# Extra products of constants ahead of the first pair's products in the recurrence's preparation

## The chip, the cores and the metric

The kernel runs on one core of a Trainium2 chip. The metric is the device time of one execution in microseconds, the median of several runs. The kernel before took 3859.59 us (median of 3 runs, 3859.28 to 3872.24).

## The reference, cut to what matters

The reference is one inference step of a two-layer trunk for 1024 prompt tokens and 8 samples of 16 tokens, 1024 features. Layer 0 is an RWKV-7 layer: projections of the mixed input, a recurrence over time per head, an output projection, then a SwiGLU feed-forward. Layer 1 is attention over a band of chunks with a second feed-forward. The change touches the recurrence alone:

```python
def step(s, inp):
    r_t, w_t, k_t, v_t, a_t, b_t = inp
    sa = jnp.einsum('bhij,bhj->bhi', s, a_t)
    s = s * w_t[:, :, None, :] + sa[..., None] * b_t[:, :, None, :] + v_t[..., None] * k_t[:, :, None, :]
    y = jnp.einsum('bhij,bhj->bhi', s, r_t)
    return s, y
```

The 1152 tokens are 3 blocks of 384. A block is 3 windows of 128 tokens (w = 0 to 8; window 8 holds the samples), and a window has 16 heads of 64, taken as two halves of 8 heads (hf = 0, 1).

## The kernel before

The step by step recurrence is computed in chunks of 64 tokens: within a chunk, products of all pairs of tokens are formed, masked, and a triangular system is solved. `proj(b)` makes the projections of block b (`proj_lora`, `proj_k`, `proj_r`, `proj_v`) and, in between, `inverses(b)`, which solves the triangular systems of its three windows. `windows(us)` runs the recurrence. Its units are taken in pairs, the two halves of one window: `prep(i)` calls `win_prep` for both units of pair i, then `win_run` runs their states, `win_y` and `win_post` make the output, and the next pair is prepared. For block b > 0, `layer0a` alternates five steps of the windows of block b-1 with four of `proj(b)` (line 1195); for the last block the windows 6, 7, 8 alternate with the output projection and the adaLN products (`ada_steps`, lines 1202 to 1206). So the first pair of a block (windows 0, 3 and 6) is prepared while the next block's `proj_lora` runs, whose gate products (`gates`, line 595, tiles `acc<-ag`) are followed by a sigmoid on ACT and a scan on DVE (line 607). Window 6's pair is prepared beside the end of block 2's `proj_v` and the first output projections.

`win_prep(w, hf)` loads the operands (XL, and BK, which has one buffer, so that the next unit's load waits until this unit has been read), and does three things on PE, all into banks called G, of which there are two. For each chunk c of 2 it takes two banks, one per row half e, and writes 4 pairwise products of 128 columns into each (line 842); DVE masks them out of the banks (lines 845, 847). Then it takes two banks more and transposes BK into them (line 856); ACT copies these to BKT (line 858). All are fp32. The operands of e = 0 lie in rows 0 to 63, those of e = 1 in rows 64 to 127.

Other names that the steps use: `acc<-mx` are the large projection products of 384 columns, `st` the banks of the solver's merges and of the states, `aux<-raw,scT` the adaLN products, whose weights (`raw<-in_wada`) come by POOL's queue, `cst` the constants' tile of 916 columns (identity, block ones, ones, masks), `st<-y,cst` the 128x512 fp32 products of `win_post` (lines 1058 and 1062), `Z<-T` and `TT<-Z` the DMAs of the solver.

The order of the instructions on an engine isn't that of the Python text: `TileContext(nc, schedule_with_timeline_sim=True)` orders them by a simulated timeline within their dependences. An instruction more at one place moves others.

Of the kernel before, what the change touches and what calls it, by code (L numbers as in the profile page):

```python
# [137 lines left out]
def mm(nc, out, lhsT, rhs, start, stop):  # L138
    return nc.tensor.matmul(out, lhsT, rhs, start=start, stop=stop)  # L139


class Trunk:
# [631 lines left out]
    def st(self, tag, shape, bufs=1, dt=F32):  # L774
        return self.pp.tile(shape, dt, tag=tag, name=self.nm(tag), bufs=bufs)

    def win_first(self, w, hf, ld):

        nc = self.nc
        b, wi = divmod(w, 3)  # L780
        fs = slice(4 * hf, 4 * hf + 4)
        pa = self.wt("pa", [128, 2, 8, 64], 1)
        for i, n in enumerate(("kk", "b")):
            nc.sync.dma_start(pa[:, i], self.sp[b][n][:, wi, fs, :].rearrange("p f (c t) -> p (f c) t", t=64))
        G = self.bank("G", 2)
        for c in range(2):
            for f in range(4):
                for e in range(2):
                    h = slice(64 * e, 64 * e + 64)
                    mm(nc, G[h, (c * 4 + f) * 64:(c * 4 + f + 1) * 64], pa[h, 1, 2 * f + c], pa[h, 0, 2 * f + c], True, True)  # L790
        aab = self.wt("Aab", [128, 8, 64], 2)
        gv = G.rearrange("p (g t) -> p g t", t=64)
        if w == 8:
            nc.vector.tensor_tensor(aab, gv, self.C("mas").rearrange("p (o t) -> p o t", o=1).broadcast_to([128, 8, 64]), ALU.mult)
        else:
            nc.scalar.activation(aab, gv, AF.Copy)
        for e in range(2):
            nc.scalar.dma_start(ld[:, hf, e], aab[64 * e:64 * e + 64])
        return aab
# [13 lines left out]
    def win_prep(self, w, hf):  # L813

        nc = self.nc
        smp = w == 8
        b, wi = divmod(w, 3)
        fs = slice(4 * hf, 4 * hf + 4)
        R = Ctx()
        src = lambda n, p0=0, p1=128: self.sp[b][n][p0:p1, wi, fs, :].rearrange("p f (c t) -> p (f c) t", t=64)  # L820
        ring, nr = (self.st, 1) if (w, hf) == (7, 1) and 1 else (self.wt, 3)
        xl = ring("XL", [128, 3, 8, 64], nr)
        bk = self.wt("BK", [128, 8, 2, 64], 1)
        nc.sync.dma_start(xl[0:64, 0], src("kk", 0, 64))
        nc.sync.dma_start(xl[64:128, 1], src("kk", 64, 128))
        nc.sync.dma_start(bk[0:64, :, 0, :], src("b", 0, 64))
        nc.sync.dma_start(bk[64:128, :, 0, :], src("k", 64, 128))
        nc.sync.dma_start(bk[0:64, :, 1, :], src("k", 0, 64))
        nc.sync.dma_start(bk[64:128, :, 1, :], src("b", 64, 128))
        nc.sync.dma_start(xl[:, 2], src("r"))  # L830
        R.eend = self.eends[b][:, fs, 2 * wi:2 * wi + (8 if smp else 2)]
        bkv = bk.rearrange("p (f c) s t -> p f c (s t)", c=2)

        yl = ring("YL", [128, 2, 2, 4, 64], nr)
        mr = self.C("mrs" if smp else "mr").rearrange("p (o t) -> p o t", o=1).broadcast_to([128, 4, 64])
        ma = self.C("mas" if smp else "ma").rearrange("p (o t) -> p o t", o=1).broadcast_to([128, 4, 64])
        for c in range(2):
            Gs = [self.bank("G", 2) for _ in range(2)]
            for f in range(4):
                for e in range(2):  # L840
                    h = slice(64 * e, 64 * e + 64)
                    mm(nc, Gs[e][:, f * 128:(f + 1) * 128], bkv[h, f, c], xl[h, e:3:2 - e, 2 * f + c, :], True, True)
            for e in range(2):
                gv = Gs[e].rearrange("p (f x t) -> p f x t", f=4, x=2)
                nc.vector.tensor_tensor(yl[:, c, e], gv[:, :, 1, :], mr, ALU.mult)
                h2 = slice(64 * (1 - e), 64 * (1 - e) + 64)
                nc.vector.tensor_tensor(xl[h2, e, c::2], gv[h2, :, 0, :], ma[h2], ALU.mult)

        bkt = ring("BKT", [128, 2, 2, 256], nr)
        pt = [self.bank("G", 2) for _ in range(2)]  # L850
        for c in range(2):
            for f in range(4):
                for e in range(2):
                    o0 = (c * 4 + f) * 64
                    h = slice(64 * e, 64 * e + 64)
                    nc.tensor.transpose(pt[e][:, o0:o0 + 64], bkv[h, f, c], self.C("ident")[h, h])
        for e in range(2):
            nc.scalar.activation(bkt[:, :, e], pt[e].rearrange("p (c f d) -> p c (f d)", c=2, f=4), AF.Copy)
        R.xl, R.yl, R.bkt, R.TT = xl, yl, bkt, self.TT.pop((w, hf))
        uv = R.uv = self.wt("UV", [128, 2, 2, 4, 64], 3)  # L860
        for c in range(2):
            for e in range(2):
                p0 = 64 * (1 - e)
                nc.sync.dma_start(uv[p0:p0 + 64, c, e], self.sv[b][wi, c * 64:(c + 1) * 64, e, 4 * hf:4 * hf + 4, :])
        return w, hf, R
# [1087 lines left out]
```

## Time and profile before

| what | value |
|---|---|
| median of the runs shown | 3859.59 us |
| the profiled execution | 3864.46 us, of which the span is 3862.7 us |
| mean granted clock of PE | 0.932 |
| PE / weight load / DVE / ACT / POOL busy | 3540.6 / 3125.0 / 2291.8 / 1575.7 / 643.2 us |
| projections and recurrence | about the first 1240 us of the span |
| pairwise products (line 842) | 328.9 to 1159.1 us, 576 MATMULs |

How to read it: the span runs from the first instruction to the last; times within it count from its start. An fp32 product appears as two MATMULs, one in fp32r as one. The granted clock is a share of PE's full clock, 1.00 or 0.50 at any moment in this trace, and in a stretch its mean. In a list of instructions the number in square brackets is the idle time of the engine before, and what ended it. A busy share counts an instruction from its start to its modelled end, so that a busy PE may still stream little.

### The profile page before, as it was taken

What the parts mean: (1) busy time and instruction counts of PE and PEld (TensorE: products, weight loads), DVE (VectorE), ACT (ScalarE), POOL (GpSimd) and SP (SyncE); (2) the same over time, 40 slices, a digit from 0 to 9 for tenths busy, and PEclk for the clock granted to TensorE, in tenths of its full rate; (3) what the DMA queues carried; (4) which work ended last, traced back from release to release, by engine and by line L of the source; (5) the groups of instructions that cost most, each with busy time, mean ns of one, the idle gap of its engine ahead of it and who ended that gap; (6) DMA issues with size and microseconds to landing.
All of it is one profiled execution on the core that took longest, in us unless ns stands there. A gap on an engine that the chain in (4) does not pass through costs nothing.

```text
span 3862.7 us, 72343 instructions
## 1 busy us (share of the span) xinstructions
PE 3540.6 (92%) x28614; PEld 3125.0 (81%) x28614; DVE 2291.8 (59%) x4420; ACT 1575.7 (41%) x2998; POOL 643.2 (17%) x564
## 2 busy tenths in 40 slices
PE   5889989989888699999999899789889799999999
PEld 4777778777666599999887879677777799999998
DVE  4666666765445764554456752666675764554567
ACT  5545646544223433333311353565654533333310
POOL 0000000000010364453000100000000254453000
PEclk8887998889798789999999999899999899999999
DMA  5775776776664412223755112454555322222521
GB/s 209 233 218 163 214 207 182 200 199 199 187 201 147 143 67 75 74 75 105 254 179 182 70 62 97 141 152 140 153 185 167 116 80 75 74 75 92 171 86 70
DMA packets 428963, 552.31 MB, mean 143 GB/s; under 512 B 128432, under 2 KB 296880, under 8 KB 424144
## 3 DMA queue, kind: packets, MB, share of 16 engines
q1 hardware_dynamic: 352640, 449.49, 36.4%
q0 software_dynamic: 21840, 79.31, 6.8%
q10 hardware_dynamic: 54144, 18.89, 2.1%
q8 instruction: 225, 3.69, 0.4%
q14 instruction: 114, 0.93, 0.1%
HBM read 413.42 MB, written 134.12 MB: 142 GB/s over the span
## 4 chain that ended last, share of the span: by engine, by line
PE 69%; DMA 9%; DVE 9%; issue 6%; ACT 5%; POOL 1%; SPq 1%; ACTq 0%; DVEq 0%; POOLq 0%
PE S L139 31%; PE PT L139 15%; PE acc L139 13%; PE st L139 3%; PE O L139 2%; PE G L139 1%; DVE h L269 1%; PE PT L1779 1%; PE aux L139 1%; DMA raw<-in_wada 1%; DMA TT<-Z 1%; DMA Z<-T 1%; DVE wlo L269 1%; PE Y L139 1%; ACT pts L1780 1%
## 5 line engine op out<-in xcount | busy, mean ns | idle before, releaser
L139 PE MATMUL S<-h,w 128*128 128x320 f32 (+1 forms) x4944 | 698.9, 300 | 18.2 <-DVE h L269 7.7
L139 PEld LDWEIGHTS S<-h,w 128*128 128x128 f32 x4944 | 676.8, 192 | 26.6 <-DVE h L269 12.8
L139 PE MATMUL acc<-mx,whi 128*128 128x384 f32 x1728 | 512.5, 374 | 41.8 <-ACT mx L268 20.2
L139 PE MATMUL S<-h,wh 128*128 128x320 f32 (+1 forms) x2844 | 529.8, 337 | 14.0 <-DVE h L1151 8.1
L139 PEld LDWEIGHTS S<-h,wh 128*128 128x128 f32 x2844 | 455.4, 189 | 70.6 <-issue 11.7
L139 PEld LDWEIGHTS acc<-mx,whi 128*128 128x128 f32 x1728 | 340.4, 205 | 74.1 <-ACT mx L268 23.9
L268 ACT ACTIVATE w<-rq 128x512 fp32r<-128x512 f32 x308 | 192.4, 629 | 503.5 <-PE S L139 203.1
L269 DVE TENSOR_TENSOR w<-rq,w 128x512 fp32r<-128x512 f32 x308 | 268.6, 875 | 199.5 <-ACT w L268 198.9
L139 PE MATMUL PT<-h,w 128*128 128x320 f32 (+1 forms) x2448 | 355.4, 300 | 14.1 <-ACT w L268 6.9
L139 PEld LDWEIGHTS PT<-h,w 128*128 128x128 f32 x2448 | 337.9, 192 | 17.8 <-ACT w L268 7.1
L139 PE MATMUL acc<-mx,wlo 128*128 128x384 f32 x864 | 318.8, 369 | 6.5 <-DVE wlo L269 6.5
L139 PE MATMUL PT<-h,wh 128*128 128x320 f32 (+1 forms) x1428 | 286.4, 344 | 10.8 <-DVE wh L269 3.9
L1338 POOL TENSOR_TENSOR t<-t,t 128x576 f32<-128x576 f32 (+1 forms) x132 | 216.5, 1641 | 417.0 <-ACT t L1345 295.3
L139 PEld LDWEIGHTS PT<-h,wh 128*128 128x128 f32 x1428 | 233.5, 190 | 41.7 <-issue 6.0
L269 DVE TENSOR_TENSOR wlo<-raw,whi 128x1024 fp32r<-128x1024 f32 x114 | 139.6, 1226 | 85.3 <-ACT whi L268 84.3
L139 PEld LDWEIGHTS acc<-mx,wlo 128*128 128x128 f32 x864 | 176.7, 205 | 16.3 <-DVE wlo L269 10.3
L269 DVE TENSOR_TENSOR h<-h,h 128x1024 fp32r<-128x1024 f32 (+4 forms) x112 | 122.9, 1111 | 89.9 <-ACT h L268 73.0
L268 ACT ACTIVATE wh<-rq 128x512 fp32r<-128x512 f32 x124 | 74.8, 625 | 242.8 <-PE S L139 160.7
L268 ACT ACTIVATE h<-h 128x1024 fp32r<-128x1024 f32 (+4 forms) x112 | 103.3, 935 | 168.1 <-DMA h<-sd 111.7
L268 ACT ACTIVATE whi<-raw 128x1024 fp32r<-128x1024 f32 x114 | 119.6, 1053 | 124.3 <-PE acc L139 78.9
L1338 DVE TENSOR_TENSOR t<-S,t 128x576 f32<-128x576 f32 (+1 forms) x116 | 86.4, 745 | 132.0 <-PE S L139 132.0
L1405 DVE TENSOR_TENSOR h<-h,S 128x640 f32<-128x640 f32 (+1 forms) x150 | 111.9, 750 | 78.8 <-PE S L139 78.7
(433 smaller groups left out, 5754.7 us busy)
## 6 DMA issues: line engine op xcount, KB each, us to landing
h<-in_wada SPq DMA_DIRECT2D x64, 512.0 KB, 6.4
rq<-in_wg SPq DMA_DIRECT2D x88, 256.0 KB, 2.6
rq<-in_wu SPq DMA_DIRECT2D x88, 256.0 KB, 2.6
rq<-in_wd SPq DMA_DIRECT2D x88, 256.0 KB, 3.0
raw<-in_wada POOLq DMA_DIRECT2D x32, 512.0 KB, 5.0
kc<-in_ck SPq DMA_DIRECT2D x16, 1024.0 KB, 5.0
vc<-in_cv SPq DMA_DIRECT2D x16, 1024.0 KB, 5.8
sd<-t SPq DMA_DIRECT2D x88, 160.0 KB, 1.9
```

What stands on the lines that cost most here:

```text
L139: return nc.tensor.matmul(out, lhsT, rhs, start=start, stop=stop)
L268: self.nc.scalar.activation(hi, x, AF.Copy)
L269: self.nc.vector.tensor_tensor(lo, x, hi, ALU.subtract)
L1338: eng.tensor_tensor(out, x, y, ALU.add)
L1405: nc.vector.tensor_tensor(y, y, d, ALU.add)
L1779: nc.tensor.transpose(pt[:, j * 128:(j + 1) * 128], P[:, j * 128:(j + 1) * 128], self.C("ident"))
L1780: nc.scalar.activation(pts[:, 0:nk * 128], pt[:, 0:nk * 128], AF.Copy)
```

## The change

A new helper `keep(ts, n)` writes n products of constants into each of the two banks `ts`: for e = 0 and 1 the left operand is rows 64e to 64e+63 of the constants' first 128 columns, the right one the same rows of their first 512 columns, so each is a 64-row fp32 product of 512 columns that fills the bank. It is called in `win_prep` right after banks are taken, for windows 0, 3 and 6 only (w % 3 == 0): with n = 1 ahead of the pairwise products of each chunk (n = 2 for window 6), and with n = 1 ahead of the transposes. Nobody reads what it writes; the real products then write over it, each with start set. That makes 6 extra products in a unit of windows 0 and 3, and 10 in one of window 6, 44 in all.

```diff
+    def keep(self, ts, n):
+
+        for _ in range(n):
+            for e, t in enumerate(ts):
+                h = slice(64 * e, 64 * e + 64)
+                mm(self.nc, t, self.cst[h, 0:128], self.cst[h, 0:512], True, True)
+
...
         for c in range(2):
             Gs = [self.bank("G", 2) for _ in range(2)]
+            if w % 3 == 0:
+                self.keep(Gs, 1 + (w == 6))
             for f in range(4):
                 for e in range(2):
...
         pt = [self.bank("G", 2) for _ in range(2)]
+        if w % 3 == 0:
+            self.keep(pt, 1)
         for c in range(2):
```

The change moves other instructions too. Three places on PE follow; in a row, the names are tiles with their numbers, the sizes those of the right operand, and xN counts equal rows. In the code of the change the lines from 784 on are 7 to 11 higher (L856 becomes L867). First, PE at the first unit of window 0 (G are its banks, `st` the end of an earlier window's merge), before and after:

```order
L139 MATMUL acc_3583<-mx_3220,whi_3592 128x384
L139 MATMUL acc_3583<-mx_3221,whi_3592 128x384
L139 MATMUL st_2426<-TT_2224,p_441_2231 32x32 x8
L139 MATMUL st_2445<-TT_2227,p_444_2271 32x32 x8
L139 MATMUL G_3262<-XL_3252,BK_3253 128x128
L139 MATMUL G_3263<-XL_3252,BK_3253 128x128
```

```order
L139 MATMUL acc_3595<-mx_3220,whi_3604 128x384
L139 MATMUL acc_3595<-mx_3221,whi_3604 128x384
L139 MATMUL st_2426<-TT_2224,p_441_2231 32x32 x8
L139 MATMUL st_2445<-TT_2227,p_444_2271 32x32 x8
L139 MATMUL G_3262<-cst 128x512
L139 MATMUL G_3263<-cst 128x512
L139 MATMUL G_3262<-XL_3252,BK_3253 128x128
L139 MATMUL G_3263<-XL_3252,BK_3253 128x128
```

The two extra products stand side by side ahead of the real ones, at the same place of the order. Second, PE at the second unit of window 0, among the gate products (`acc<-ag`), before and after:

```order
L139 MATMUL acc_3716<-ag_3574,whi_3705 128x384
L139 MATMUL acc_3716<-ag_3574,wlo_3706 128x384
L139 MATMUL G_3326<-XL_3316,BK_3317 128x128 x4
L139 MATMUL G_3327<-XL_3316,BK_3317 128x128 x4
L139 MATMUL acc_3722<-ag_3573,whi_3705 128x384
L139 MATMUL acc_3722<-ag_3573,wlo_3706 128x384
L139 MATMUL acc_3729<-ag_3574,whi_3705 128x384
L139 MATMUL acc_3729<-ag_3574,wlo_3706 128x384
L139 MATMUL G_3340<-XL_3316,BK_3317 128x128 x4
```

```order
L139 MATMUL G_3332<-cst 128x512
L139 MATMUL G_3333<-cst 128x512
L139 MATMUL G_3332<-XL_3322,BK_3323 128x128 x4
L139 MATMUL G_3333<-XL_3322,BK_3323 128x128 x4
L139 MATMUL acc_3728<-ag_3586,whi_3717 128x384
L139 MATMUL acc_3728<-ag_3586,wlo_3718 128x384
L139 MATMUL G_3348<-cst 128x512
L139 MATMUL G_3348<-XL_3322,BK_3323 128x128 x4
L139 MATMUL acc_3734<-ag_3585,whi_3717 128x384
L139 MATMUL acc_3734<-ag_3585,wlo_3718 128x384
L139 MATMUL G_3349<-cst 128x512
```

After the first bank pair, the extra products stand one by one between the gate products, and the unit comes one gate product earlier. Third, PE at the end of window 6's first unit and the start of its second (banks G_11212 and on before, G_11246 and on after), before and after:

```order
L856 MATMUL G_11104<-cst,BK_11066 128x64 x8
L139 MATMUL st_11284<-UV_11124,XL_11065 64x64
L856 MATMUL G_11105<-cst,BK_11066 128x64 x8
L139 MATMUL G_11212<-XL_11202,BK_11203 128x128 x4
L139 MATMUL acc_11183<-mx_11129,whi_11179 128x384
L139 MATMUL acc_11183<-mx_11130,whi_11179 128x384
L139 MATMUL aux_11193<-raw_11194,scT 32x256 x4
```

```order
L139 MATMUL G_11136<-cst 128x512
L867 MATMUL G_11136<-cst,BK_11090 128x64 x8
L139 MATMUL st_11328<-UV_11158,XL_11089 64x64
L139 MATMUL G_11137<-cst 128x512
L867 MATMUL G_11137<-cst,BK_11090 128x64 x8
L139 MATMUL G_11246<-cst 128x512 x2
L139 MATMUL acc_11217<-mx_11163,whi_11213 128x384
L139 MATMUL aux_11227<-raw_11228,scT 32x256 x4
L139 MATMUL G_11247<-cst 128x512 x2
L139 MATMUL acc_11217<-mx_11164,whi_11213 128x384
```

The first real product of the second unit, which waits for BK, no longer stands right behind the transposes: four extra products, a projection product and adaLN products stand there. Through the rest of the recurrence merges, gate products and loads change places with each other; from the feed-forward on the order is the same but for a few rows. POOL's queue has one load in another place.

## The prediction

> **What bounds the kernel now.** I read the page first, then the busy table of the stretches that the change touches, then the instructions of PE in those stretches, then the chain of waits there. The page says that PE is busy nearly all the time and that its clock is not always full:
>
> ```profile
> span 3862.7 us, 72343 instructions
> PE 3540.6 (92%) x28614; PEld 3125.0 (81%) x28614; DVE 2291.8 (59%) x4420; ACT 1575.7 (41%) x2998; POOL 643.2 (17%) x564
> PEclk8887998889798789999999999899999899999999
> PE 69%; DMA 9%; DVE 9%; issue 6%; ACT 5%; POOL 1%; SPq 1%; ACTq 0%; DVEq 0%; POOLq 0%
> ```
>
> The first thirteen digits of the clock line, some 1250 us, are the recurrence, and its 7s and 8s are where the clock was at half for part of a slice. The extra products stand in three of these places, the preparation of windows 0, 3 and 6. The busy table cuts them by stage (columns: stretch, its length, busy time of PE, weight load, DVE, ACT and POOL, the granted clock, DMA):
>
> ```profile
> 328.00:345.00 17.00, 16.63 (x166) 13.63 (x162) 12.05 (x39) 7.55 (x13) 1.59 (x3) 1.00 0.57 146
> 345.00:350.00 5.00, 3.93 (x22) 3.13 (x22) 4.96 (x10) 4.69 (x10) 0.53 (x1) 0.79 0.59 113
> 350.00:365.00 15.00, 14.86 (x53) 10.74 (x52) 14.01 (x28) 10.35 (x19) 0.53 (x1) 0.50 0.54 176
> 365.00:375.00 10.00, 8.26 (x38) 6.96 (x37) 8.88 (x19) 6.98 (x11) 0.53 (x1) 0.67 0.80 221
> 375.00:400.00 25.00, 23.77 (x383) 20.84 (x383) 13.71 (x28) 7.70 (x17) 1.05 (x2) 0.52 0.67 176
> 640.00:665.00 25.00, 25.00 (x460) 20.98 (x460) 13.65 (x26) 16.72 (x32) 3.19 (x6) 1.00 0.47 134
> 665.00:680.00 15.00, 13.99 (x80) 10.46 (x77) 12.90 (x32) 10.14 (x22) 0.00 (x0) 0.51 0.54 141
> 680.00:705.00 25.00, 24.35 (x98) 20.38 (x99) 21.02 (x49) 12.38 (x20) 1.58 (x3) 0.54 0.63 191
> 977.00:991.00 14.00, 13.78 (x115) 11.52 (x114) 8.24 (x26) 3.03 (x7) 0.00 (x0) 0.58 0.45 121
> 991.00:996.00 5.00, 0.15 (x1) 0.18 (x2) 2.51 (x7) 0.41 (x1) 0.00 (x0) 0.50 0.63 166
> 996.00:1018.00 22.00, 21.18 (x102) 13.79 (x103) 12.15 (x30) 4.50 (x9) 1.57 (x3) 0.52 0.82 228
> ```
>
> What to see: in all three places the clock falls to a half when the gate products meet the first pair's products, and stays there for some 40 to 50 us although PE is busy throughout. At 350 to 365 PE is busy 14.86 of 15 us at clock 0.50, but DVE is busy 14.01 of 15 us as well: a full clock would buy little there. At 375 to 400 DVE has 13.71 of 25 us, and PE alone is the limit. At 991 to 996 PE stands still.
>
> **The price of one extra product.** No fp32 product of 64 rows by 512 columns is in the trace. Its neighbours are a 128-row product of 512 columns, and the pairwise products with 128 columns each, where four make 512 columns:
>
> ```profile
> 946.60 0.51 PE L139 MATMUL acc<-mx,whi 128*128 128x384 f32 x2
> 947.12 0.51 PE L139 MATMUL acc<-mx,whi 128*128 128x384 f32 x2
> 947.48 1.02 PE L139 MATMUL st<-y,cst 128*128 128x512 f32 x2
> 948.51 0.51 PE L139 MATMUL acc<-mx,whi 128*128 128x384 f32 x2
> 328.85 1.16 PE L139 MATMUL G<-XL,BK 64*128 64x128 f32 x16
> 329.94 0.45 PE L139 MATMUL acc<-mx,wlo 128*128 128x384 f32 x1
> 976.72 1.16 PE L139 MATMUL G<-XL,BK 64*128 64x128 f32 x8
> 977.80 0.69 PE L139 MATMUL st<-TT,p 32*32 32x32 f32 x16
> 980.56 2.07 PE L139 MATMUL G<-XL,BK 64*128 64x128 f32 x8
> 982.56 0.47 PE L139 MATMUL st<-UV,XL 128*64 128x64 f32 x2
> ```
>
> An fp32 product counts as two MATMULs. From 947.48 to 948.51 lie one product of 512 columns and one of 384 (the wlo, row left out here); three of those take 0.52 us (946.60 to 947.12), so 0.17 each, and the 512-column product takes 1.03 - 0.17 = 0.86 us at full clock. Four products of 128 columns on one half of the rows take 977.80 - 976.72 = 1.08 us at full clock and 982.56 - 980.56 = 2.00 us at half. Eight that alternate between the two row halves take 329.94 - 328.85 = 1.09 us, no more than four on one half: the halves run side by side. So I call a slot the time of one extra product, or of two that stand next to each other on different halves. A slot costs 0.86 us (at most 1.08) at full clock and 2.00 us (at least 1.72, twice 0.86) at half. I take 0.86, since the extra products mostly stand between full-row products.
>
> **The change part by part.** By the order on PE there are 44 extra products: 12 for window 0, 12 for window 3, 20 for window 6. In windows 0 and 3 only the first two of a unit stand side by side, so that a unit is 5 slots; in window 6 the two on one bank follow each other, and none is beside its partner: 20 slots.
>
> First units (hf 0) of windows 0 and 3: before, PE was busy 16.63 of 17 us and 25.00 of 25 us there, at clock 1.00. Nothing hides the slots, and the path runs over PE. Cost: 2 x 5 x 0.86 = +8.6 us (at most 10.8).
>
> Second units (hf 1) of windows 0 and 3: they lie among the gate products, where the clock falls. The extra products stream on both halves just where PE waited or ran thin products, and I expect the clock to stay full until the unit is through. PE's work at full clock is then, in 345 to 365, 3.93 x 0.79 + 14.86 x 0.50 = 10.5 us, and 4.3 us of slots, 14.8 in all; DVE's 18.97 us of 20 become the limit and cover the slots. Gain: 1.0 us. In 665 to 680: PE 13.99 x 0.51 + 4.3 = 11.4 us, under DVE's 12.90 of 15 us. Gain: 2.1 us.
>
> After these units no extra product follows: the second pair's preparation (windows 1 and 4) has none. I take it that the clock falls at its first thin stretch, and 365 to 400 and 680 to 705 stay as they are: 0. If the clock held there too, 365 to 375 would shrink to DVE's 8.88, 375 to 400 to DVE's 13.71 (PE would need 23.77 x 0.52 = 12.4), 680 to 705 to DVE's 21.02: 1.1 + 11.3 + 4.0 = 16.4 us less. That is the lower bound of this term.
>
> Window 6: in 977 to 991 PE's 13.78 us at clock 0.58 would be 8.0 at full clock; ten slots add 8.6, together 16.6 against 14: +2.6 us. The idle stretch, 991 to 996, is a wait for the second unit's load, as the next row and the second one, from the chain, show; four extra products stand ahead of the waiting ones and run in it for nothing. In 996 to 1018 PE's 21.18 us at 0.52 become 11.0, and six slots add 5.2: 16.2 against 22, a gain of up to 5.8 us. But the chain there runs through loads on POOL's queue, not over PE:
>
> ```profile
> 995.85 2.04 PE L139 MATMUL G<-XL,BK 64*128 64x128 f32 x8 [5.07 <-DMA BK<-sp_k]
> 978.71 22.17 issue
> 1000.89 4.98 DMA raw<-in_wada
> 1005.92 10.60 issue
> 1016.53 6.92 DMA raw<-in_wada
> ```
>
> Those loads wait for buffers that PE's products free, so that a faster PE pulls them forward only in part: I take half, -2.9 us. POOL's own order hardly changes, and the waits that the first extra product of a bank has (the bank being free) are those that the first real product had.
>
> Sum: 8.6 - 1.0 - 2.1 + 2.6 - 2.9 = +5.2 us. The profiled execution took 3864.46 us (span 3862.7), 4.87 above the median of 3859.59; put on the median, the forecast is 3864.8 us, 0.13% slower. A change of 0.5%, 19.3 us, is about what a measurement of this kernel can tell from no change, so this is no change.
>
> [...]
>
> **The rivals.** First, faster: the clock holds to the end of all three places. For it: the reordering also moves merges of window 1 between the gates, and 375 to 400 has a PE limit that a full clock removes. Against it: no extra products stand there, and waits as short as the next two rows' stood just before the clock fell at 345 to 350 and, in the first of the second pair's preparation, inside 365 to 375:
>
> ```profile
> 346.07 0.44 PE L139 MATMUL acc<-ag,whi 128*128 128x384 f32 x1 [1.44 <-ACT e L605]
> 366.85 1.13 PE L139 MATMUL G<-XL,BK 64*128 64x128 f32 x8 [1.74 <-DMA BK<-sp_k]
> ```
>
> Time: 5.2 - 16.4 - 2.9 = -14.1, 3845.5 us; if the first units' slots were also covered, -22.7, 3836.9 us.
>
> Second, slower: the clock is not moved. The second units' slots and those of window 6 then run at half clock on a PE that has no free time (14.86 of 15; in 665 to 705 the chain is PE almost alone):
>
> ```profile
> by line: PE acc L139 40.5%; PE G L139 26.4%; PE st L139 6.7%; DMA Z<-T 6.6%; PE G L856 6.4%; DMA BK<-sp_k 5.4%; ACTq L883 2.4%; DVE e L625 1.3%; issue 1.2%; SPq L827 1.1%; SPq L826 1.1%; DVE YL L845 0.7%; DVE XL L847 0.7%; DVE T L880 0.5%
> ```
>
> Price: 8.6 + 2 x 5 x 2.00 + 16 x 2.00 (window 6 without the four in the wait) = +60.6, 3920 us. It decides where the clock at about 348 and 666 still falls to 0.5; in a milder form half of these 26 slots run at half clock, at the lower 1.72 us, and half of the 6.0 us of gains above stays: 8.6 + 22.4 - 3.0 = +28.0, 3887.6 us.
>
> Third, the planner's moves decide: it also moves gate products, merges and loads against each other through all of the recurrence, though their number is the same. Nothing in the profile prices that; +10 or -10 us, 3875 or 3855, is what one more or one less wait like the 5.07 us for BK at two places makes. That the change does nothing can be left out: the 44 products stand in the order.
>
> **How the numbers follow.** The forecast has 0.56, all of it within 0.5%. The first rival has 0.24, of which 0.18 lies beyond 0.5%. The second has 0.14, nearly all in its milder form, all beyond 0.5%. The third has 0.06, of which 0.02 is faster and 0.04 slower by more. So faster 0.20, same 0.62, slower 0.18. The range reaches from 3842, under the first rival's 3845.5, to 3888, the second's milder form, and leaves out about a tenth at either end: 3842 to 3888.
>
> **What would show it.** Right: 44 extra fp32 products near 0.9 us a slot; clock 1.00 through window 0's second unit, some 10 us longer than before, and DVE, not PE, without idle time there; half clock again in window 1's preparation; window 0's gates starting about 4 us late; no 5 us gap on PE before the second unit of window 6. Wrong: clock 0.5 in those units (the second rival), or 1.00 up to 400 and 705 with the stretches 10 us shorter (the first).

## The result and the profile after

The changed kernel takes 3910.81 us (median of 4 runs, 3897.04 to 3914.09) against 3859.44 us of the kernel before in the same series; the ratio is 1.0119, with a 95% interval of 1.0095 to 1.0142. It is slower by 37 to 55 us where no change was forecast, and outside the range. In what follows, differences are (ratio - 1) times the median of the kernel before in the same series.

The profiled execution after took 3897.04 us. Its page, in the lines that were shown of before (span, busy time, granted clock in 40 slices, the chain by engine):

```profile
span 3895.3 us, 72525 instructions
PE 3562.3 (91%) x28702; PEld 3123.0 (80%) x28702; DVE 2293.5 (59%) x4420; ACT 1573.3 (40%) x2998; POOL 641.9 (16%) x564
PEclk8887989698799689999999999999999899999999
PE 67%; DMA 12%; DVE 9%; ACT 5%; issue 5%; SPq 1%; POOL 1%; ACTq 0%; DVEq 0%; POOLq 0%
```

The mean clock is 0.932 as before, and the clock line has sixes where there were sevens and eights. PE is busy 21.7 us longer, and idle (span less PE's busy time) 333.0 us instead of 322.1. The stretches of the prediction (the columns as there):

```profile
345.00:350.00 5.00, 2.22 (x9) 0.91 (x8) 4.96 (x12) 3.50 (x7) 0.00 (x0) 1.00 1.03 186
350.00:365.00 15.00, 15.00 (x86) 10.07 (x89) 12.55 (x27) 6.09 (x12) 0.53 (x1) 0.52 0.44 129
375.00:400.00 25.00, 25.00 (x224) 20.73 (x223) 11.35 (x20) 9.61 (x18) 0.53 (x1) 0.53 0.37 118
680.00:705.00 25.00, 21.87 (x82) 13.98 (x79) 19.15 (x44) 11.44 (x22) 0.53 (x1) 0.60 0.39 109
```

From 350 to 365 us, in the second unit of window 0, the clock is 0.52 (0.50 before): it isn't held there. PE's instructions at that place, and at the second unit of window 3, show what stands ahead of the fall (start, duration, form, and in brackets the idle time before and what ended it):

```profile
345.08 0.34 PE L139 MATMUL acc<-ag,wlo 128*128 128x384 f32 x1
347.05 1.61 PE L139 MATMUL G<-cst 64*128 64x512 f32 x4 [1.62 <-ACT BKT L869]
349.81 2.46 PE L139 MATMUL G<-XL,BK 64*128 64x128 f32 x16 [1.15 <-DMA BK<-sp_k]
352.20 0.69 PE L139 MATMUL acc<-ag,whi 128*128 128x384 f32 x1
...
353.13 2.07 PE L139 MATMUL G<-cst 64*128 64x512 f32 x2
355.00 1.91 PE L139 MATMUL G<-XL,BK 64*128 64x128 f32 x8
```

```profile
685.91 2.56 PE L139 MATMUL G<-cst 64*128 64x512 f32 x4 [3.13 <-ACT BKT L869]
```

The extra products wait for a bank that ACT still empties (1.62 and 3.13 us), and the gate products queue behind them: in the first place none starts on PE between 345.08 and 352.20 us. The clock is at half from 350.6 us here and from 685.1 us there, and a slot that took 0.97 us (two side by side, 327.03 to 328.00) takes 1.87 us (353.13 to 355.00).

So the first reading was the prediction's second rival, slots at half clock on the path. It accounts for the places of the products; it doesn't account for this: the gates' scans of window 0's stretch are 7 us late at the first and 27 us late at the eighth and last (353.94 against 347.18 us, 397.89 against 371.15), while window 2's merges reach PE 19 us early (361.49 against 380.07). Something else had moved. The experiments separate the two.

### The profile page after: what moved, and what is told of

It reads as the page before. It is cut to its first block, busy times and chain, and to the rows that moved or that the text cites. A ratio compares the mean times of both kernels' runs of the same rounds, so it can differ in the third digit from the quotient of the medians.

```text
span 3895.3 us, 72525 instructions
## 1 busy us (share of the span) xinstructions
PE 3562.3 (91%) x28702; PEld 3123.0 (80%) x28702; DVE 2293.5 (59%) x4420; ACT 1573.3 (40%) x2998; POOL 641.9 (16%) x564
## 3 DMA queue, kind: packets, MB, share of 16 engines
q1 hardware_dynamic: 352640, 449.49, 35.9%
## 4 chain that ended last, share of the span: by engine, by line
PE 67%; DMA 12%; DVE 9%; ACT 5%; issue 5%; SPq 1%; POOL 1%; ACTq 0%; DVEq 0%; POOLq 0%
PE S L139 31%; PE PT L139 15%; PE acc L139 10%; PE st L139 3%; PE G L139 2%; PE O L139 2%; DVE h L269 1%; PE PT L1790 1%; PE aux L139 1%; DMA raw<-in_rw_o 1%; DVE wlo L269 1%; DMA sp_k<-rr 1%; DMA raw<-in_wada 1%; PE Y L139 1%; DMA yg<-y 1%
## 5 line engine op out<-in xcount | busy, mean ns | idle before, releaser
L139 PE MATMUL acc<-mx,whi 128*128 128x384 f32 x1728 | 502.6, 369 | 46.9 <-ACT mx L268 22.9
```

## The experiments

**Products in one window alone.** The condition on the window is changed, here and at the transposes, and nothing else:

```diff
-            if w % 3 == 0:
+            if w == 0:          # e1_w0; w == 3: e2_w3; w == 6: e3_w6
                 self.keep(Gs, 1 + (w == 6))
```

> Extra products in window 0 only, 12 of the 44. Prices from the changed kernel's trace: 0.97 us a slot at full clock, 1.87 us at half. Theory 1 (the products' own PE time decides; the second unit runs at half clock on the path): 5 x 0.97 + 5 x 1.87 = +14 us against the kernel before, 3873 to 3876 us, with the clock at 0.5 from about 350 to 398 us as in the changed kernel. Theory 2 (the reordering of gate products and merges decides, not the products' time): the changed kernel's outputs of block 0 were 28 us late but its projections at 620 us only 7 us, so +28 us if the loss comes here and is given back by chance, +7 us if not; the order on PE of this kernel is that of the changed kernel in block 0 only. If the loss of the three places does not add, this run together with the next two will not sum to the changed kernel's +46 us of the medians.

> Extra products in window 3 only, 12 of the 44. Theory 1 (their own PE time): as for window 0, +14 us, 3873 to 3876 us. Theory 2 (reordering): the order on PE stays close to that of the kernel before, so less than +5 us, and no gate product queued for over 3 us behind an extra product that waits for its bank near 686 us. The changed kernel's own milestones put 12 to 27 us on this block.

> Extra products in window 6 only, 20 of the 44. Theory 1 (their own PE time): 16 slots outside the wait for BK, of which half at full clock and half at half clock, 8 x 0.97 + 8 x 1.87 = +23 us, 3880 to 3885 us. Theory 2 (reordering): the order on PE is nearly that of the kernel before, so the products lie partly in waits and the time is within +8 us. The changed kernel's milestones rise by 13 to 28 us in this block.

Measured: window 0 alone +57.2 us (ratio 1.0148, 1.012 to 1.0177), window 3 alone +38.6 us (1.0100, 1.0081 to 1.0118), window 6 alone +17.0 us (1.0044, 1.0027 to 1.0061). The first two miss every figure that was expected of them, and the third lies between its two. Their sum, 113 us, is more than twice the 46 us of all three together, and twelve products in window 0 alone cost no less than all 44 (46 to 68 us against 37 to 55). No price for a product gives that. Each of these kernels has an order of its own; window 6's is the closest to the order before, and it alone lies near its products' own time (20 slots of 0.97 us make 19.4).

**Thin products.** 16 columns instead of 512, all 44, the planner free:

```diff
-                mm(self.nc, t, self.cst[h, 0:128], self.cst[h, 0:512], True, True)
+                mm(self.nc, t[:, 0:16], self.cst[h, 0:128], self.cst[h, 0:16], True, True)
```

> All 44 extra products stay where the change puts them, but each has 16 columns instead of 512, so that it takes next to no PE time and still waits for its bank. Theory 1 (their own PE time): 20 slots at about 0.1 us, +2 us, within 0.2% of the kernel before. Theory 2 (the wait for a bank in front of the gate products and the planner's other order decide): +20 us or more, though the planner, which is told a smaller cost, lays out an order about half way between the two kernels'.

Measured: +37.9 us (1.0098, 1.0060 to 1.0136). With the products' PE time nearly gone (PE is busy 3534.9 us, 5.7 less than before) most of the loss is still there. Theory 1 falls as the whole cause.

**Order and products apart.** The order of issue of each engine can be written down from one kernel and imposed on another, by an edge from each instruction to the next on its engine that sets the order alone:

```diff
+def pin(tc, extra):
+    ins = [i for i in tc.nc.cur_bb.bb.instructions if i.name not in extra]
...
+        for x, y in zip(s, s[1:]):
+            tc.add_manual_dep(ins[int(y)], ins[int(x)].name, mybir.DependencyInfo(mybir.DependencyClass.NoSync, mybir.DependencyReason.DATA))
...
         Trunk(tc, a, o).build()
+        pin(tc, KEPT)
```

`s` is the engine's order, `extra` the names of the extra products, which stay free. In the traces PE's other products follow the imposed order but for a few rows. The edges themselves cost little: a kernel further down (x1_w03) has them and 24 extra products and takes 5.0 us more (-1.2 to +11.2). That gives the two missing corners of a square, and with thin products a third:

> The kernel before, without any extra product, but with every engine's instructions pinned in the order that they have in the changed kernel (edges that set the order of issue alone and add no wait). The computation is that of the kernel before. Theory 1 (the extra products' own PE time makes the changed kernel slower): within 5 us of the kernel before, about 3862 us. Theory 2 (the planner's other order does): +25 to +45 us, 3885 to 3905 us, with the same work on PE and more idle time or more half clock.

> The changed kernel with all 44 extra products in full size, but all other instructions of every engine pinned in the order of the kernel before; the extra products stand directly ahead of the first product of their bank. Theory 1 (their own PE time): their work is 23 us at full clock by the changed kernel's trace, so +23 us if they run at full clock outside of waits, up to +45 us with half of them at half clock: 3885 to 3907 us. Theory 2 (the order): under +12 us, since the places in the old order leave waits in which they run. If the clock were held by them, as the forecast had it, the half clock of 347 to 365 and 665 to 703 us would shrink here, and the time would be below 3862 us.

> The extra products have 16 columns instead of 512, all engines pinned in the order of the changed kernel, so that only the extra products' PE time is gone and their wait for a free bank stays. Theory 1: within 7 us of the kernel before. Theory 2: as the kernel without them in the same order, +25 to +45 us. If the wait for a bank ahead of queued products costs by itself, it is slower than that kernel by 5 us or more; the difference to the changed kernel (about +46 us in the medians) is then what the products' PE time is worth in this order.

Measured, beside the changed kernel:

| | no products | thin products | 44 products |
|---|---|---|---|
| order of the kernel before | 0 | | r2_prods +35.9 us (1.0071 to 1.0116) |
| order of the changed kernel | r1_order +33.6 us (1.0070 to 1.0104) | r3_thin +36.3 us (1.0067 to 1.0121) | +45.9 us (1.0095 to 1.0142) |

The order alone makes about 34 us, without one extra product; the wait for a bank, kept in the thin kernel, adds nothing that can be told from zero (+2.7 us, with intervals of some 7 to 10 us either way). Theory 2 holds for the order, but its other half fails: the products are not cheap in the old order. And the two costs don't add: 33.6 + 35.9 = 69.5 against 45.9. The pages show where the time goes (spans and PE of the kernel with the order alone, then of that with the products alone):

```profile
span 3904.9 us, 72356 instructions
PE 3547.9 (91%) x28614; PEld 3132.0 (80%) x28614; DVE 2293.0 (59%) x4420; ACT 1573.7 (40%) x2998; POOL 642.4 (16%) x564
```

```profile
span 3887.7 us, 72515 instructions
PE 3561.0 (92%) x28702; PEld 3120.7 (80%) x28702; DVE 2293.1 (59%) x4420; ACT 1573.8 (40%) x2998; POOL 642.7 (17%) x564
```

With the new order alone PE is idle 3904.9 - 3547.9 = 357.0 us, 35 more than before; with the products alone 326.7 us, 5 more. The other traces fall into the same two groups. In the six kernels that run a new order with thin products or none PE is idle 344.3 (the nudge, below) to 364.9 us (r3_thin); in the six that are pinned to the old order it is 324.8 to 334.9, however many products they have. So in these traces a new order is paid in idle time, and the products in busy time. In the changed kernel, which has both, the idle time is 333.0: by these traces its products fill some 24 us of what its order opens, which would be why the two don't add. That figure is rough, since each trace is one execution (the changed kernel's is the fastest of its four, that of the order alone the slowest of its six).

What the order does in block 0: the scans of the gates (line 607) on DVE, in stretches of 15 us, first in the kernel before, then with the order alone (columns: stretch, length, busy time and count, clock, DMA):

```profile
350.00:365.00 15.00, 4.77 (x5) 0.50 0.54 176
365.00:380.00 15.00, 1.91 (x2) 0.61 0.81 236
380.00:395.00 15.00, 0.00 (x0) 0.50 0.63 146
395.00:410.00 15.00, 0.00 (x0) 0.86 0.52 165
```

```profile
350.00:365.00 15.00, 0.94 (x1) 0.61 0.52 132
365.00:380.00 15.00, 2.84 (x3) 0.50 0.34 101
380.00:395.00 15.00, 2.88 (x3) 0.50 0.36 117
395.00:410.00 15.00, 0.94 (x1) 0.78 0.43 127
```

And PE's instructions with the order alone, at the place where the gates were:

```profile
354.00 0.69 PE L139 MATMUL acc<-ag,whi 128*128 128x384 f32 x1 [0.75 <-DVE kp L650]
...
366.08 0.74 PE L139 MATMUL st<-TT,p 32*16 32x16 f32 x58
368.59 0.73 PE L139 MATMUL st<-TT,p 32*16 32x16 f32 x64 [1.77 <-ACT p L906]
371.86 0.36 PE L139 MATMUL st<-t,Aab 32*32 32x32 f32 x3 [2.54 <-ACT TT L917]
```

Eight scans belong to this stretch, the first of them before 350 us in the kernel before. There they were through by 380 us and the merges (`st`) came after them. In the new order merges of window 2 stand between the gates; steps of a merge wait for ACT or DVE to copy the step before out of its bank (1.77 us for p and 2.54 us for TT on ACT in the rows above, 0.18 us for t on DVE at 360.49 us), and the gates behind them on PE wait too. In these stretches the clock is low in both (0.50 to 0.61 from 350 to 395 us), so the clock isn't the main thing that makes the gates late: other work and waits stand ahead of them. PE is idle 4.6 us from 325 to 405 us before and 11.0 with the order alone. The longest waits there are, before and with the order alone (what waited, for what: us in total, times, longest):

```profile
PE G L139 <- DMA BK<-sp_k: 1.7, 1, 1.7
PE acc L139 <- ACT e L605: 1.4, 1, 1.4
PE G L856 <- DVE XL L847: 0.6, 1, 0.6
PE st L139 <- DVE t L900: 0.6, 3, 0.2
```

```profile
PE G L856 <- DVE XL L847: 3.4, 3, 1.9
PE st L139 <- ACT TT L917: 2.5, 1, 2.5
PE G L139 <- DMA BK<-sp_k: 2.3, 2, 1.9
PE st L139 <- ACT p L906: 1.8, 1, 1.8
```

No single wait is large. How much of the 34 us each of the three blocks keeps can't be read off exactly, since a late block is partly made up by the next; in its profiled execution the kernel is 36 us late in layer 0's feed-forward (the same product starts at 1458.1 us against 1422.3), and PE has been idle 30 us more by then.

**Is it this order, or any new order?** Two thin products (under 0.3 us by the author's estimate; 16 of the 512 columns of a 0.97 us slot would be 0.03 us each) ahead of the first bank pair of window 0's first unit; and the orders of two earlier kernels without their products.

```diff
-            if w % 3 == 0:
-                self.keep(Gs, 1 + (w == 6))
+            if w == 0 and hf == 0 and c == 0:
+                self.keep(Gs, 1)            # 16 columns
...
-        if w % 3 == 0:
-            self.keep(pt, 1)
```

> Two extra products of 16 columns only, ahead of the first pairwise products of window 0's first unit, under 0.3 us of PE time; nothing pinned. The planner answers them with an order on PE that differs from that of the kernel before as much as it does from the changed kernel's. Theory 1 (what counts is where the extra products stand and how long they run): within 5 us of the kernel before. Theory 2 (any new order of the planner's costs, whatever causes it): +20 to +45 us.

> No extra product; every engine pinned in the order that the planner gives the kernel with extra products in window 0 only, which took 57 us longer than the kernel before. Theory (the order is the cost): most of it remains, +35 to +55 us. Rival (the 12 products are the cost): within 10 us of the kernel before.

> No extra product; every engine pinned in the order that the planner gives the kernel with extra products in window 3 only, which took 38 us longer than the kernel before. Theory (the order is the cost): +25 to +38 us. Rival (the 12 products are the cost in this order, though in the old order they and those of window 0 cost 5 us together): within 10 us of the kernel before.

Measured: the nudge +12.8 us (1.0033, 1.0017 to 1.0050), between its two expectations, which both miss. The order of the window 0 kernel +33.3 us of its 57.2 (1.0086, 1.0069 to 1.0104), that of the window 3 kernel +22.0 us of its 38.6 (1.0057, 1.0037 to 1.0077): the larger part each time, a little less than expected, and the products add 24 and 17 us in those orders (each difference is uncertain by 11 to 13 us). So five new orders were timed in all (with the changed kernel's own and the thin kernel's), each slower, by 13 to 38 us; a new order has no fixed price.

**The products in the old order, place by place.** All of these are pinned to the order before. Only the condition differs; a bank gets one product, and in window 6 two ahead of the pairwise products, as in the change:

```diff
+            if w in (0, 3):                              # x1_w03
+            if w in (0, 3) and hf:                       # x2_hf1
+            if w in (1, 4) or w in (0, 3) and hf:        # x3_pairs
+            if w == 6 and not hf:                        # x4_w6hf0
+            if w == 6 and hf:                            # x5_w6hf1
```

> Full-size extra products for windows 0 and 3 only (24 of the 44), all other instructions pinned in the order of the kernel before. In the pinned kernel with all 44 the clock held through both second units and the milestones were 5 us late after window 3 and 2 us late at 965 us. Theory 1 (order, and the products of window 6): within 6 us of the kernel before, as the forecast's own terms for these windows had it (8.6 - 1.0 - 2.1 = +5.5 us). Theory 2 (the products cost their own time everywhere): 10 slots at 0.97 us and 10 at 1.87 us, +28 us.

> Full-size extra products for the second units of windows 0 and 3 only (12), all other instructions pinned in the order of the kernel before. If these alone hold the clock through their units, the forecast's terms give -1.0 - 2.1 = -3.1 us, 3858 us, with the clock at 1.00 to about 365 and 684 us. If the first units' products are needed for it, the clock falls at about 348 and 666 us as before, and 10 slots at 1.87 us make +19 us.

> Full-size extra products for the second units of windows 0 and 3 and for both units of windows 1 and 4 (36), all other instructions pinned in the order of the kernel before, to see whether the clock can be held to the end of the thin stretch and what that is worth. If it holds to 400 and 705 us and PE is the limit there: -3.1 - 16.4 = -19.5 us, 3842 us. If it holds but DVE, ACT and the loads are the limit: within 5 us of the kernel before. If it falls all the same: 20 slots more at up to 1.87 us, +20 to +37 us.

> Full-size extra products for the first unit of window 6 only (10), all other instructions pinned in the order of the kernel before. The forecast gave +2.6 us for this unit (ten slots of 0.86 at full clock against what the full clock saves). In the pinned kernel with all 44, the load that follows this unit went out 6 us late, of which 2.5 us came from before. Theory 1 (the forecast's term holds): +2 to +5 us. Theory 2 (what window 6 costs lies here): +10 us or more.

> Full-size extra products for the second unit of window 6 only (10), all other instructions pinned in the order of the kernel before. The forecast gave 0 for the four in the wait for BK and -2.9 us for the rest, at full clock. In the pinned kernel with all 44 this unit ran at half clock (1001 to 1049 us), with six slots of about 1.9 us on the path over PE. Theory 1 (forecast): -3 to +2 us. Theory 2 (second rival, in this place alone): 6 x 1.87 = +11 us.

| run | us | interval of the ratio |
|---|---|---|
| x1_w03 | +5.0 | 0.9997 to 1.0029 |
| x2_hf1 | +11.6 | 1.0011 to 1.0049 |
| x3_pairs | +34.4 | 1.0057 to 1.0120 |
| x4_w6hf0 | +7.7 | 1.0004 to 1.0036 |
| x5_w6hf1 | +10.1 | 1.0014 to 1.0037 |

Windows 0 and 3 together cost +5.0 us, and the forecast's terms for them were +5.5. With all 44 products in the old order the clock does what the forecast said in window 0, and for part of window 3; the busy table of that kernel (r2_prods) and three of its products on PE:

```profile
345.00:365.00 20.00, 18.78 (x107) 12.04 (x104) 18.56 (x40) 16.10 (x31) 1.05 (x2) 1.00 0.49 150
365.00:385.00 20.00, 14.78 (x70) 12.09 (x70) 14.09 (x29) 10.49 (x17) 0.53 (x1) 0.74 0.82 228
665.00:685.00 20.00, 18.30 (x117) 11.61 (x116) 18.20 (x43) 13.24 (x25) 0.53 (x1) 0.98 0.56 148
685.00:705.00 20.00, 19.35 (x61) 13.52 (x60) 11.11 (x28) 8.37 (x13) 0.53 (x1) 0.50 0.35 116
```

```profile
349.12 1.13 PE L142 MATMUL G<-cst 64*128 64x512 f32 x4
...
353.83 1.09 PE L142 MATMUL G<-cst 64*128 64x512 f32 x2 [0.49 <-DVE XL L859]
...
683.51 1.54 PE L142 MATMUL G<-cst 64*128 64x512 f32 x2 [1.19 <-DVE XL L859]
```

In window 0 the clock is full through the whole second unit (1.00) and falls at 370 us, after it. PE is busy 18.78 of 20 us there and DVE 18.56, so the row doesn't tell which of them is the limit. In the changed kernel the extra products of the first bank pair stand behind 1.62 us of idle time and the pairwise ones after them behind 1.15 us, and the clock fell under the latter (349.81 us, the fall at 350.6); here both follow gate products without idle time, the next extra products come after 0.49 us, and the clock stays full. The products do this, not the pinning: with products in window 6 alone the same stretch, 345 to 365 us, has 0.58 (x4_w6hf0). In window 3 the row of 665 to 685 us holds the rest of the first unit and the start of the second. Before the change, too, the second unit begins late in it, with this product behind its load:

```profile
679.84 3.06 PE L139 MATMUL G<-XL,BK 64*128 64x128 f32 x16 [1.01 <-DMA BK<-sp_k]
```

In r2_prods that unit's extra products begin at 675.39 us, and the clock falls at 684.0, in the middle of the unit, with the product behind 1.19 us of idle time; the rest of the unit runs at half clock (0.50 from 685 to 705 us).

Window 6 is the place where the forecast's terms fail in the old order too. In its second unit the four products in the wait are followed by six at half clock (r2_prods, PE):

```profile
1005.80 3.78 PE L142 MATMUL G<-cst 64*128 64x512 f32 x4
1017.79 3.78 PE L142 MATMUL G<-cst 64*128 64x512 f32 x4
...
1030.75 2.07 PE L142 MATMUL G<-cst 64*128 64x512 f32 x2
```

With the products of this unit alone (x5_w6hf1), the busy table of its stretch, two rows of before and then three with these products:

```profile
990.00:1005.00 15.00, 9.11 (x45) 6.75 (x44) 11.28 (x29) 3.24 (x6) 1.04 (x2) 0.50 0.67 190
1020.00:1035.00 15.00, 12.01 (x126) 8.87 (x118) 6.10 (x13) 4.45 (x10) 1.06 (x2) 0.77 0.76 190
```

```profile
990.00:1005.00 15.00, 14.20 (x39) 7.28 (x39) 9.63 (x25) 3.21 (x6) 1.05 (x2) 0.50 0.74 198
1005.00:1020.00 15.00, 15.00 (x55) 8.74 (x54) 4.48 (x11) 0.76 (x3) 0.00 (x0) 0.50 0.65 175
1020.00:1035.00 15.00, 15.00 (x71) 7.03 (x72) 2.09 (x4) 3.19 (x7) 1.05 (x2) 0.50 0.59 153
```

PE, which stood idle or ran faster there before, is the limit throughout, at half clock, and six slots of 1.87 us make 11.2 us: +10.1 measured. That is the second rival's mechanism, in this place alone. The first unit costs +7.7 us (interval +1.5 to +13.9), for a term of +2.6.

The two kernels that were to use the held clock don't gain. With the second units alone (x2_hf1, +11.6 us, between its two expectations) window 0 held it for the most part; in window 3 it had fallen at 662.1 us, before the first extra product there (672.26). With the second pairs as well (x3_pairs) the clock fell at 365 us and stayed down:

```profile
345.00:365.00 20.00, 15.69 (x75) 10.25 (x75) 18.37 (x37) 13.87 (x27) 0.53 (x1) 0.92 0.69 221
665.00:685.00 20.00, 20.00 (x66) 12.79 (x66) 15.05 (x38) 13.09 (x26) 0.53 (x1) 0.50 0.50 144
```

```profile
345.00:365.00 20.00, 17.73 (x88) 10.28 (x86) 18.86 (x37) 14.31 (x28) 1.05 (x2) 1.00 0.63 173
365.00:385.00 20.00, 18.85 (x65) 14.71 (x66) 14.15 (x30) 7.58 (x12) 0.53 (x1) 0.50 0.58 170
385.00:405.00 20.00, 18.35 (x334) 12.10 (x334) 6.61 (x14) 4.41 (x11) 0.53 (x1) 0.50 0.43 103
```

So the bound of -16.4 us, the clock held to the end of the thin stretch, isn't to be had this way, and no version tried is faster than the kernel before.

## Why the prediction was wrong, point by point

**Two steps failed**, and each alone takes the time out of the range: 3859.6 + 33.6 = 3893.2 us with the new order alone, 3859.6 + 35.9 = 3895.5 with the products alone (of which those of windows 0 and 3 make 5.0); the range ends at 3888. **The first step is the planner's order**, the third rival, "the planner's moves decide". The prediction saw that the order changes ("it also moves gate products, merges and loads against each other through all of the recurrence"), wrote "Nothing in the profile prices that", gave it nothing in the sum, and put it at 10 us either way with a chance of 0.06. Alone it makes +33.6 us (27 to 40), in idle time of PE. The forecast priced each product in the places of the order before, and took those places as given.

**Window 6 is the second step**: +2.6 and -2.9 us in the sum. The "gain of up to 5.8 us" in its second unit rested on a full clock after a 5 us wait; the clock stayed at half (0.50 from 990 to 1035 us in x5_w6hf1), PE became the limit, and -2.9 us is +10.1. The term of +2.6 for the first unit is +7.7, whose interval, +1.5 to +13.9, holds it.

**The clock through the second units** ("I expect the clock to stay full until the unit is through") was right for window 0 in the order that it was worked out from (1.00), and half right for window 3, where it fell in the middle of the unit. The prediction took 665 to 680 us for window 3's second unit; by the row at 679.84 that is the rest of the first. In the changed kernel's own order it was wrong (0.52 and 0.60 in the rows above): there PE stood idle just ahead of the extra products (1.62 and 3.13 us). The tell that the prediction named for the second rival, clock 0.5 in those units, did come, but that rival's price, 60.6 us of slots, isn't what was paid: without any slot the same order costs 33.6 us.

**The wait for a bank** was taken to be the one that the first real product had. In the changed kernel it is 1.62 and 3.13 us, with gate products behind it; but the thin products, which keep it, add nothing that can be told from zero.

**The price of a slot** was right in kind and a little low: 0.97 us at full clock against 0.86, and 1.87 at half, where the prediction said 2.00, at least 1.72. A first unit had four slots, not five: in the changed kernel both its bank pairs stand side by side (at 327.03 and 333.97 us in window 0).

**The sum for windows 0 and 3**, +8.6 - 1.0 - 2.1 = +5.5 us, came out in the old order: +5.0 us (-1.2 to +11.2). That doesn't bear out its parts: the interval would have held -1 as well as +11, the 2.1 us belong to a stretch that was misread, and no run measured the first units or the gains by themselves. So the sum may be right by luck.

**Nothing after the units** was right: the clock falls again (at 370 us in r2_prods), and twelve products in each second pair don't hold it (0.50 from 365 to 405 us in x3_pairs).

**What stays open.** The parts in the old order sum to 5.0 + 7.7 + 10.1 = 22.8 us against 35.9 (27 to 45) for all 44 at once; the intervals of the parts, some 6 us each, leave room for that, and no run tells whether there is more. By the difference of the two kernels, 35.9 - 5.0 = 30.9 us, window 6's products cost more beside the others than its two units do alone. Why the planner's new orders are worse on the chip than the old one was not tried, nor why the nudge costs a third of what the others do.

## What to carry to other kernels

Where a scheduler orders the program, an instruction added at one place is two changes, the instruction and a new order, and the second can cost more: price it by pinning the old order and adding the instruction, and by pinning the new order and leaving it out. In these traces extra products went with a full clock where they stood ahead of the fall with at most 0.49 us of idle time before them (window 0 in the old order), but also behind 1.13 and 1.62 us (679.02 and 347.05 us in the changed kernel, where the clock fell at 685.1 and 350.6); behind 1.19 us (683.51 us in r2_prods) they came with the fall, at 684.0, and behind 3.13 us (685.91 us in the changed kernel) after it, and were paid at half clock. So the idle time ahead is what was seen beside the fall, not a rule that these runs show. Where PE was the limit at half clock, in window 6's second unit, the extra products cost about their full time (11.2 us for six slots, +10.1 measured).

## What the runs showed of the hardware

In x2_hf1 the clock stayed at half on a PE that was never idle: from 665 to 685 us PE is busy 20.00 of 20 us at 0.50 (the row above). The clock had fallen at 662.1 us, in the first unit of window 3, as it did before the change (at 665.4). In x1_w03, which adds the first units' products and nothing else, it stayed full until 686.1 us (1.00 from 665 to 685 us). That speaks for those products, but it is one trace each, and in x3_pairs, which lacks them too, it fell only at 682.3 (0.93 from 665 to 685 us).

The time wanders more than one profiled pair shows. In the series of x1_w03 the kernel before took 3851.1 to 3881.3 us over 29 runs, while its first three runs lay within 13 us, so that single traces of these kernels (x4_w6hf0's span is 3861.1 us, under that of before, with a ratio of 1.0020) don't give the sign of a few us; the ratios do.
